# A batched matmul whose TensorE loop is aligned to a code block and given one empty first turn

## The chip, the cores and the metric

One core of one Trainium2 (trn2) chip. The metric is device time in microseconds (us) of one execution; lower is better. PE is TensorE and PEld its weight load, DVE is VectorE, ACT is ScalarE, POOL is GpSimd, SP issues the transfers; a q after a name (PEq, SPq) is the engine's sequencer, whose records are its branches, register operations and waits. The span is the time from the first to the last instruction of the profiled run. PSUM is the memory that PE's results go to here. The clock in a window is the share of PE's full clock that was granted. A block is what one packet of queue 8 brings, 16,384 bytes of code in these traces.

## The reference

```python
def reference(x, weight):      # x: 8 x 16 x 256 x 512, weight: 8 x 16 x 512 x 384, float32
    return np.matmul(x, weight).astype(np.float32)
```

128 independent products. 168 MB are read and 50 MB written.

## The kernel before

The batches are done in 32 groups of four. For each group SP loads x and the weights in float32, ACT casts x to bf16, DVE casts the weights in eight pieces, PE transposes x (16 instructions), DVE copies the transposed x out of PSUM, PE multiplies in four quarters of 32 matmuls each, ACT copies each quarter out, SP stores. Everything is synchronised with counting semaphores, and the engines run loops of their own, PE with two groups a turn. Cut to what the change and the argument touch:

```python
G = 4; T = 4; XS, WS, OS = 2, 4, 4; PT, PO = 4, 2; LAG = 4; BIAS = 8   # T quarters, PO accumulators

def load(e, t, U, s):                       # SP; group n = t*U + s
    n = t * U + s
    if not isinstance(n, int) or n >= XS:
        e.wait_ge(x_cast, n + (1 - XS))     # ACT's cast has freed the x buffer
    e.dma_start(x_sb[s % XS][:], ...)
    ...                                     # two halves of the weights, each after a wait on w_cast

def prepare(e, t, U, s):                    # DVE
    ...                                     # 8 weight casts, then T copies x_t <- pt

def multiply(e, t, U, s):                   # PE
    n = t * U + s
    e.wait_ge(x_cast, n + 1)
    for q in range(T):
        e.wait_ge(t_copied, n * T + (q + 1 - PT + BIAS))
        ...                                 # 4 transposes
    e.wait_ge(w_cast, n * (G * S) + G * S)
    for q in range(T):
        e.wait_ge(t_copied, n * T + (q + 1 + BIAS))
        e.wait_ge(o_copied, n * T + (q + 1 - PO + BIAS))
        ...                                 # 32 matmuls, then p_made += 1

def on_tensor(e):
    U = 2
    e.sem_inc(t_made, BIAS); e.sem_inc(p_made, BIAS)
    e.wait_ge(id_done, 2)
    with e.Fori(0, NG // U) as t:           # 16 turns
        for s in range(U):
            multiply(e, t, U, s)

def on_scalar(e):                           # copies of quarters 0, 1; cast of the next x; copies 2, 3
    ...
```

## Time and profile before

| | kernel before |
|---|---|
| time, median of 3 runs | 519.71 us (519.63 to 519.82) |
| span of the profiled run | 518.0 us |
| transfers | 218.16 MB, mean 421 GB/s, in the middle 428 to 429 |
| PE, DVE, ACT busy | 61%, 63%, 41% |
| code fetched for PE after the start (queue 8) | 2 packets of 16 KiB, at 29.2 and 37.9 us |

Transfers take the whole span, no engine is busy over two thirds of it. The prediction below shows the lines. In order of time: start, duration, engine, line, operation, count, and in brackets the idle time before and what ended it.

```profile
8.89 3.70 ACT L130 CAST x_bf<-x_sb 128x2048 bf16<-128x2048 f32 x2 [6.28 <-DMA x_sb<-in_x_dram]
12.56 7.86 DVE L148 CAST w_bf<-w_sb 64x1536 bf16<-64x1536 f32 x8 [12.56 <-DMA w_sb<-in_weight_dram]
...
12.72 3.68 PE L167 MATMUL pt<-identity,x_bf 128*128 128x128 f32 x16 [12.72 <-ACT x_bf L130]
```

PE's first transposes start 0.13 us after ACT's first cast ends (8.89 + 3.70). PE isn't late.

### The profile page before, as it was taken

Reading aid. Unit: us, or ns where it says so; the run is one execution under the profiler, and the core shown is the slowest. Engines: PE = TensorE matmul, PEld = TensorE weight load, DVE = VectorE, ACT = ScalarE, POOL = GpSimd, SP = SyncE. Lnnn points to the kernel's source line nnn. Section 1 sums busy time; section 2 is a strip of 40 time slices with the busy share of each in tenths; the row PEclk is TensorE's granted clock in tenths of the full one; section 3 lists DMA queues with packets and bytes.
Section 4 is the critical chain, followed back from the end, with each engine's and each line's share of the span. In section 5 each row is a group of like instructions: output and inputs, shape, how many; then the busy total and the mean of one; then the engine's idle time right before and its main releaser. Section 6 shows DMA issues by size and latency. Waiting matters only on the chain.

```text
span 518.0 us, 11228 instructions
## 1 busy us (share of the span) xinstructions
PE 315.0 (61%) x4608; PEld 198.0 (38%) x4608; DVE 323.9 (63%) x384; ACT 212.8 (41%) x193; POOL 0.7 (0%) x6
## 2 busy tenths in 40 slices
PE   0685775476655676555756557665566655675654
PEld 0453443343433443333434334343344333343432
DVE  0878867655577555775556765557755577555670
ACT  3073643455234552335542345423455234553242
POOL 0000000000000000000000000000000000000000
PEclk9798976888668776868786687768777787878687
DMA  8999999999999999999999999999999999999995
GB/s 337 430 424 428 426 429 427 430 428 427 430 429 426 431 425 430 428 430 432 426 427 429 430 433 425 427 430 428 432 429 427 427 430 430 430 429 424 432 428 229
DMA packets 18868, 218.16 MB, mean 421 GB/s; under 512 B 2096, under 2 KB 2096, under 8 KB 2608
## 3 DMA queue, kind: packets, MB, share of 16 engines
q1 hardware_dynamic: 18864, 218.11, 99.2%
q8 instruction: 2, 0.03, 0.0%
q14 instruction: 2, 0.02, 0.0%
HBM read 167.77 MB, written 50.33 MB: 421 GB/s over the span
## 4 chain that ended last, share of the span: by engine, by line
DMA 82%; DVE 13%; issue 2%; PE 2%; SPq 1%; ACT 0%; DVEq 0%
DMA w_sb<-in_weight_dram 82%; DVE w_bf L148 13%; PE po L181 2%; SPq L108 0%; SPq L100 0%; ACT out_sb L195 0%; DVE x_t L154 0%; DVEq L143 0%; DVEq L225 0%; SPq L287 0%; SPq L54 0%
## 5 line engine op out<-in xcount | busy, mean ns | idle before, releaser
L148 DVE CAST w_bf<-w_sb 64x1536 bf16<-64x1536 f32 x256 | 244.4, 955 | 179.4 <-DMA w_sb<-in_weight_dram 172.3
L181 PE MATMUL po<-w_bf,x_t 128*32 128x384 bf16 x4096 | 233.5, 402 | 122.2 <-DVE x_t L154 122.2
L195 ACT COPY out_sb<-po 128x768 f32<-128x768 f32 x128 | 99.4, 803 | 291.0 <-PE po L181 291.0
L181 PEld LDWEIGHTS po<-w_bf,x_t 128*32 128x32 bf16 x4096 | 125.8, 117 | 227.0 <-DVE x_t L154 131.7
L167 PE MATMUL pt<-identity,x_bf 128*128 128x128 f32 x512 | 81.5, 322 | 73.4 <-ACT x_bf L130 73.4
L130 ACT CAST x_bf<-x_sb 128x2048 bf16<-128x2048 f32 x64 | 118.5, 1902 | 6.3 <-DMA x_sb<-in_x_dram 6.3
L167 PEld LDWEIGHTS pt<-identity,x_bf 128*128 128x128 f32 x512 | 72.2, 212 | 85.2 <-issue 85.2
L154 DVE COPY x_t<-pt 128x1024 bf16<-128x1024 bf16 x128 | 79.5, 682 | 1.0
L130 ACT ACT_TABLE_LOAD x1 | 1.3, 1283 | 1.3 <-PEq L231 1.3
masks.py:199 POOL TENSOR_SCALAR_AFFINE_SELECT identity<-identity 128x128 f32<-128x128 f32 x1 | 0.3, 293 | 0.2 <-POOL identity L201 0.2
L201 POOL MEMSET identity<- 128x128 f32 x1 | 0.2, 205 | 0.5 <-SPq L54 0.5
L276 POOL MEMSET const-uint8-127<- 128x1 uint8 x1 | 0.1, 103 | 0.0
L276 POOL MEMSET const-bfloat16-1.0<- 128x1 bf16 x1 | 0.1, 102 | 0.0
L276 POOL MEMSET const-float32-0.0<- 128x1 f32 x1 | 0.1, 99 | 0.2 <-issue 0.2
L276 POOL MEMSET const-float32-1.0<- 128x1 f32 x1 | 0.1, 99 | 0.0
## 6 DMA issues: line engine op xcount, KB each, us to landing
w_sb<-in_weight_dram SPq DMA_DIRECT2D x64, 1536.0 KB, 27.6
x_sb<-in_x_dram SPq DMA_DIRECT2D x32, 2048.0 KB, 25.9
out_dram<-out_sb SPq DMA_DIRECT2D x31, 1536.0 KB, 30.5
out_dram<-out_sb SPq DMA_DIRECT2D x4, 384.0 KB, 4.1
```

The source lines that it names most:

```text
L130: ins = e.copy(out=x_bf[s % BS][:, :, h], in_=x_sb[s % XS][:].rearrange("p r (q s c) -> p r s q c", s=S, c=KO)[:, :, h],)
L148: e.tensor_copy(out=w_bf[(s * G + d * D + a) % WBS][h * HP : (h + 1) * HP], in_=w_sb[slot][a * HP : (a + 1) * HP, h * KO : (h + 1) * KO, : ...
L154: e.tensor_copy(out=x_t[s % TS][:, 2 * q : 2 * q + 2], in_=pt[(s * T + q) % PT][:].bitcast(bf16),).then_inc(t_copied, 1)
L167: ins = e.transpose(pt[(s * T + q) % PT][:, rr, h, :], words[:, 2 * q + rr, h :: KO // 2], identity[:],)
L181: ins = e.matmul(po[(s * T + q) % PO][mine, rr, :N], x_t[s % TS][:, 2 * q + rr, ko // 2, mine, ko % 2], w_bf[(s * G + i) % WBS][:, ko, :], ...
L195: e.copy(out=out_sb[s % OS][:, 2 * q : 2 * q + 2, :], in_=po[(s * T + q) % PO][:, :, :N],).then_inc(o_copied, 1)
L201: e.memset(identity[:], 0.0).then_inc(id_done, 1)
L276: nc = _bacc.Bacc("TRN2", target_bir_lowering=False, num_devices=1)
```

## The change

The intent is that PE's code lies at a known place (the loop head at slot 0 of a block, as the call asks) and that the loop's last block has been fetched before the work starts: one more turn, the first, skips both bodies and only jumps through. Since the counter now starts one later, all counts move by LEAD = 2 groups.

```diff
-    BIAS = 8
+    BIAS = 16
+    LEAD = 2
...
-            e.wait_ge(x_cast, n + (1 - XS))
+            e.wait_ge(x_cast, n + (1 - XS + LEAD))
...                                     (w_cast, t_copied, o_copied shifted too; multiply split
                                         into transpose and multiply, the latter one quarter q a call)
     def on_vector(e):
+        e.sem_inc(w_cast, LEAD * G * S)
     def on_scalar(e):
+        e.sem_inc(x_cast, LEAD)
...
-        e.wait_ge(id_done, 2)
-        with e.Fori(0, NG // U) as t:
-            for s in range(U):
-                multiply(e, t, U, s)
+        pe = mybir.EngineType.PE
+        with nc.Fori(
+            0, NG // U + 1, engines=OrderedEngineSet([pe]), head_slot={pe: 0}
+        ) as t:
+            with e.If(t > 0):
+                e.wait_ge(id_done, 2)
+                for s in range(U):
+                    transpose(e, t, U, s)
+                    for q in range(T if s == 0 else T // 2):
+                        multiply(e, t, U, s, q)
+            with e.If(t > 0):
+                for q in range(T // 2, T):
+                    multiply(e, t, U, U - 1, q)
```

## The prediction

The clock that it calls full in the group at 33.55 us was 1.00 (33.5 to 39 us).

> **What bounds the kernel now.** I read the slices first, then the chain that ended last, then the waits, then the order in time of one group of four batches, and the sequencer's records in the trace last.
>
> ```profile
> DMA  8999999999999999999999999999999999999995
> GB/s 337 430 424 428 426 429 427 430 428 427 430 429 426 431 425 430 428 430 432 426 427 429 430 433 425 427 430 428 432 429 427 427 430 430 430 429 424 432 428 229
> ```
>
> The transfers are busy in every slice, at a rate that hardly moves from slice 2 to slice 39. Only the first and the last slice are lower. The same by stage (columns: window, its length, busy time and count of PE, PEld, DVE, ACT, POOL, granted clock, DMA share, GB/s):
>
> ```profile
> 0.00:30.00 30.00, 11.77 (x144) 7.46 (x144) 15.04 (x18) 9.22 (x7) 0.70 (x6) 0.89 0.94 390
> ...
> 238.00:490.00 252.00, 155.43 (x2232) 97.06 (x2228) 161.94 (x192) 103.11 (x95) 0.00 (x0) 0.76 1.01 429
> 490.00:518.00 28.00, 14.31 (x232) 8.37 (x224) 10.12 (x12) 9.13 (x10) 0.00 (x0) 0.80 0.80 337
> ```
>
> The page counts 218.16 MB in all. At about 428.5 GB/s, the rate of the middle, they take 509 us, and the span is 518.0 us. The other 9 us are at the two ends: 30 us at 390 GB/s lose 30 x (1 - 390/428.5) = 2.7 us, and 28 us at 337 lose 6.0 us. No change of TensorE's code can get at the 509, and the nine left are 1.7% of the time.
>
> The chain that ended last says the same:
>
> ```profile
> DMA 82%; DVE 13%; issue 2%; PE 2%; SPq 1%; ACT 0%; DVEq 0%
> ```
>
> PE's 2% is one piece, 8.12 us from 502.48 us, the matmuls of the last group after the last weights. In all other groups PE isn't on it. What PE itself waits for:
>
> ```profile
> PE po L181 <- DVE x_t L154: 122.2, 32, 4.8
> PE pt L167 <- ACT x_bf L130: 73.4, 32, 12.7
> ```
>
> Each of the 32 groups has two waits, for data both times: the transposes (L167) for ScalarE's cast of x, the matmuls (L181) for VectorE's first copy of x_t, which stands behind the weight casts and so behind the weights' transfer. Two groups in order of time, which are one turn's second half and the next turn's first:
>
> ```profile
> 278.80 7.30 PE L181 MATMUL po<-w_bf,x_t 128*32 128x384 bf16 x128 [4.25 <-DVE x_t L154]
> ...
> 281.60 0.80 ACT L195 COPY out_sb<-po 128x768 f32<-128x768 f32 x1 [8.81 <-PE po L181]
> ...
> 284.25 3.70 ACT L130 CAST x_bf<-x_sb 128x2048 bf16<-128x2048 f32 x2
> 286.04 7.86 DVE L148 CAST w_bf<-w_sb 64x1536 bf16<-64x1536 f32 x8 [5.50 <-DMA w_sb<-in_weight_dram]
> ...
> 288.08 2.64 PE L167 MATMUL pt<-identity,x_bf 128*128 128x128 f32 x16 [1.99 <-ACT x_bf L130]
> ```
>
> The loop's back edge lies between 286.10 (278.80 + 7.30) and 288.08 us. PE idles 1.99 us there, and ScalarE's cast ends at 287.95, 0.13 us before the transposes. In the middle of a turn, where there is no branch, the gap is the same (1.98 us before the transposes at 271.52). So the back edge costs nothing today.
>
> [...]
>
> ```profile
> q8 instruction: 2, 0.03, 0.0%
> q14 instruction: 2, 0.02, 0.0%
> ```
>
> Queue 8 moved two packets of 16,384 bytes, at 29.2 us (1,061 ns) and 37.9 us (1,108 ns), the end of the first and of the second group. I take them to be PE's[...]. [...] a turn has 32 x 2 instructions of transposes, 256 x 2 of matmuls and some 21 others, about 597[...], yet nothing is fetched on queue 8 after 39 us in 15 more turns. The loop is resident already. [...] here the loop's compare-and-branch takes 208 to 224 ns taken and 76 not taken (the last), so I use these. [...]
>
> **The change, part by part.** The order of the transposes and matmuls doesn't change at all: a turn still does group 2t and group 2t+1, and only the last two quarters of the odd group's matmuls stand in a block of their own behind a second test. DVE, ACT and SP have the same instructions and the same waits; the constants (BIAS 16, LEAD 2) only shift counts for a counter t that starts one later, and two semaphore increments at the start set them.
>
> *Alignment.* Loop head at slot 0 instead of somewhere: 7 instructions longer, about 604[...]. It was resident before, so 0 us in the steady state.
>
> *The first, empty turn.* It tests twice, counts, and jumps back: four instructions, and perhaps one or two fetches. [...] PE stood ready at 1.86 us (its first register operation), and its first transposes wait for x until 12.7 us. Two fetches of 1.1 us and four branches of 0.2 us are an estimated 3 us of 10.8 us free. On the path: 0.
>
> *What it saves.* The fetches at 29.2 and 37.9 us. The second falls into the second group's matmuls, 5.38 us from 33.55; two groups on, at 59.02, with no fetch, they take 5.38 too. The first falls before transposes that wait for ScalarE (cast ends at 30.96, transposes at 31.09). So both are hidden today: saved 0.
>
> *The tests inside a turn.* Per turn I count seven more sequencer instructions: compare-and-branch and a branch twice, two register operations more for the second block's waits, and one semaphore wait for the identity. One follows another about 0.1 us apart in the trace, 0.28 us after a taken branch. Five come between the second and third quarter: an estimated 0.4 to 0.75 us. There the sequencer is held in any case: the third quarter waits until ScalarE has emptied the first of the two accumulators. In the group shown it asked at 281.77 and was released at 282.43, and the quarter's first matmul came at 283.33. In the group at 33.55, when the clock was full: 35.15, 35.92, 36.16. In the last group, the only one where PE is on the chain: 505.46, 506.18, 507.58. So 0.66 to 0.77 us of waiting to take it up, plus 1.4 us of lead in the group that counts. Path: 0, at most 0.1. The remaining ones lie at the back edge, where the sequencer is done at 285.24 and waits until 287.95: 2.7 us free, some 0.5 needed.
>
> *Sum.* 0 to 0.1 us in the last group, 0 elsewhere: 519.7 + 0.05, about 519.8.
>
> **Rivals.** *The loop gets fetched again in each turn*[...]. Three blocks of 16 KiB in 16 turns are 0.79 MB, 1.8 us at 428.5 GB/s, and three stalls of 1.1 us per turn on PE. PE has 2 us before the transposes and up to 4.8 before the matmuls, so most of it stays hidden: some 521.5 us; all of it on the path would be 16 x 3.3 = 53 us more. Against it: the kernel before does not refetch with a head at an arbitrary slot, and the body is hardly longer.
>
> *The fetch is worth something*, in timed runs or by a chain that I don't see: at most its two packets, 2.2 us, so 517.5. Against it: neither is beside an idle stretch of PE that ends late.
>
> *PE's small delays reach the transfers.* There is a way: matmuls, ScalarE's copies, its next cast of x, and only then the issue of the next load of x, for which the queue waits long:
>
> ```profile
> SPq L100 <- ACT x_bf L130: 259.1, 30, 10.2
> ```
>
> But a weight load is issued 27.6 us (median) before it lands, while its 1.57 MB need 3.7 us: over 20 us of other transfers are queued ahead. A delay of 0.5 us shortens the queue and doesn't empty it. At the worst it adds to the last group: 520.3.
>
> **Range and chances.** The three times of before lie within 0.2 us. All mechanisms on the path give 0 to 0.1 us, the rivals -2.2 and +0.6 to +1.8; I put 8 of 10 on 518.8 to 520.8. Faster by 2% means 509.3, which is the transfer time alone without either end: 1%. Slower by 2% means 10.4 us more, 0.65 us on the path in each turn, which only steady refetching could do: 2%.
>
> **What would show it.** After the change: GB/s the same in the middle slices; DMA again some 82% of the chain; some 116 instructions more on PE (16 x 7 + 4) in a total of 11,228 before; packets of queue 8 in the first 12 us instead of at 29 and 38 us, and none later; the transposes again 1.9 to 2.0 us after the matmuls before them, released by ScalarE; the last group's matmuls 8.1 us. I am wrong if queue 8 has packets in each turn, if "PE pt" waits for issue rather than for ScalarE, if a gap over 0.2 us opens between the last group's second and third quarter, or if slices in the middle fall under 424 GB/s.

## The result, and the profile after

519.76 us median (519.50 to 520.07, four runs) against 519.67 us of the kernel before in the same rounds (519.47 to 519.82). The ratio is 1.0002, with a 95% interval of 0.9985 to 1.0020. The two are the same.

The page of the kernel after: the transfers by slice, the fetch queue and the chain that ended last.

```profile
DMA  8999999999999999999999999999999999999995
GB/s 332 427 428 426 428 427 429 431 429 424 430 432 428 431 425 430 429 430 429 428 428 431 425 434 428 427 427 430 431 432 425 429 429 430 431 428 426 431 428 233
...
q8 instruction: 3, 0.05, 0.0%
...
DMA 78%; DVE 13%; PE 3%; issue 3%; SPq 1%; ACT 1%; DVEq 0%; ACTq 0%
```

The rate is what it was. DMA's share of the chain is 78% where the prediction had some 82% again. Queue 8 moved three blocks, at 6.2, 11.8 and 17.3 us, and none later; the third missed the first 12 us that were forecast. PE's waits after (us in total, times, longest):

```profile
PE po L187 <- DVE x_t L157: 119.5, 31, 4.4
PE pt L170 <- ACT x_bf L133: 59.9, 31, 2.0
PE pt L170 <- issue: 15.0, 1, 15.0
```

31 of the 32 transposes still wait for ACT. One doesn't, the first, which waits for PE's own sequencer. The start, in order of time:

```profile
9.93 3.70 ACT L133 CAST x_bf<-x_sb 128x2048 bf16<-128x2048 f32 x2 [7.23 <-DMA x_sb<-in_x_dram]
...
13.85 7.86 DVE L151 CAST w_bf<-w_sb 64x1536 bf16<-64x1536 f32 x8 [13.85 <-DMA w_sb<-in_weight_dram]
14.98 3.27 PEld L170 LDWEIGHTS pt<-identity,x_bf 128*128 128x128 f32 x16 [14.98 <-issue]
14.99 3.47 PE L170 MATMUL pt<-identity,x_bf 128*128 128x128 f32 x16 [14.99 <-issue]
...
22.48 8.25 PE L187 MATMUL po<-w_bf,x_t 128*32 128x384 bf16 x128 [4.02 <-DVE x_t L157]
```

Two things differ from before. ACT's cast ended at 13.63 and the transposes began at 14.99, 1.36 us late. And x itself came 1.04 us later (cast at 9.93, was 8.89), the weights 1.29 us later (13.85, was 12.56). The sequencer's own records in the trace, which no view of the page lists, show the cause of the first (start and duration in ns):

```
 1979  6561  COMPARE_BRANCH  first test of the empty turn
 8598  5516  COMPARE_BRANCH  second test
14172    42  ALU_OP          count
14275   229  COMPARE_BRANCH  back to the head
14656    77  COMPARE_BRANCH  first test of the first real turn (falls through)
```

The empty turn took over 12 us, nearly all of it in two jumps. A packet of queue 8 lies within each (6.22 to 7.19 and 11.79 to 12.78 us), so I read them as waits for a target that wasn't in yet. The turn was hidden by what PE would have waited for in any case: the weight casts end at 13.85 + 7.86 = 21.71 us, and the matmuls start only after them, with 4.02 us of idle time on PE.

The second has a cause that the landings show. Each transfer leaves 16 reports of landing in the trace (2,096 for 131 transfers), and the kernel waits for all 16; I take them as one from each of the 16 DMA engines that the page counts. For the first load of x, fifteen reports came by 8.53 us and the last at 8.86 in the kernel before; in the kernel after fifteen came by 8.68 and the last at 9.91. For the first weights after, fourteen came by 12.39, and two at 13.58 and 13.82. One fetch (6.22 us, 965 ns long) had gone by before the first, two before the second. The second load of x, after the third fetch, has three late reports (thirteen by 20.97, then 22.16, 22.23 and 22.24). So each packet of code seems to hold one engine, each time another, for its 1 us (965 to 1,006 ns), and every load in flight waits for that engine. That is a reading, as the trace names no engine.

### The profile page after: what moved, and what is told of

It is laid out like the page before. It is cut to its first block, busy times and chain, and to the rows that moved or that the text cites. A ratio compares the mean times of both kernels' runs of the same rounds, so it can differ in the third digit from the quotient of the medians.

```text
span 517.9 us, 11305 instructions
## 1 busy us (share of the span) xinstructions
PE 315.2 (61%) x4608; PEld 197.7 (38%) x4608; DVE 323.9 (63%) x384; ACT 212.6 (41%) x193; POOL 0.7 (0%) x6
## 2 busy tenths in 40 slices
DMA packets 18869, 218.18 MB, mean 421 GB/s; under 512 B 2096, under 2 KB 2096, under 8 KB 2608
## 4 chain that ended last, share of the span: by engine, by line
DMA 78%; DVE 13%; PE 3%; issue 3%; SPq 1%; ACT 1%; DVEq 0%; ACTq 0%
DMA w_sb<-in_weight_dram 78%; DVE w_bf L151 13%; PE po L187 3%; ACT x_bf L133 0%; DVE x_t L157 0%; SPq L111 0%; SPq L103 0%; ACT out_sb L201 0%; SPq L110 0%; DVEq L232 0%; ACTq L131 0%; DVEq L146 0%; DVEq L156 0%; ACTq L200 0%; SPq L305 0%
## 5 line engine op out<-in xcount | busy, mean ns | idle before, releaser
L187 PE MATMUL po<-w_bf,x_t 128*32 128x384 bf16 x4096 | 232.5, 401 | 119.6 <-DVE x_t L157 119.5
L187 PEld LDWEIGHTS po<-w_bf,x_t 128*32 128x32 bf16 x4096 | 124.3, 117 | 224.8 <-DVE x_t L157 129.1
L170 PE MATMUL pt<-identity,x_bf 128*128 128x128 f32 x512 | 82.7, 325 | 74.9 <-ACT x_bf L133 59.9
L170 PEld LDWEIGHTS pt<-identity,x_bf 128*128 128x128 f32 x512 | 73.4, 213 | 86.8 <-issue 86.8
```

The lines of the kernel that those rows point to most:

```text
L170: ins = e.transpose(pt[(s * T + q) % PT][:, rr, h, :], words[:, 2 * q + rr, h :: KO // 2], identity[:],)
L187: ins = e.matmul(po[(s * T + q) % PO][mine, rr, :N], x_t[s % TS][:, 2 * q + rr, ko // 2, mine, ko % 2], w_bf[(s * G + i) % WBS][:, ko, :], ...
```

## The experiments

The ones that edit the kernel after are compared with the kernel before too; the result found these two the same.

**Alignment alone.** The kernel before, with only the loop call changed.

```diff
-        with e.Fori(0, NG // U) as t:
+        with nc.Fori(0, NG // U, engines=OrderedEngineSet([pe]), head_slot={pe: 0}) as t:
```

> The kernel before with its TensorE loop aligned to slot 0 of a block, no empty turn and no tests in the turn. Theory (the transfers set the time, PE's code placement is hidden): 519.7 us, within 0.8; no compare-and-branch over 0.3 us; the first transposes start within 0.2 us of the end of ScalarE's first cast; two or three 16 KiB packets on queue 8, all after 12 us or so, none later in the loop. Rival (alignment does something by itself which the empty turn then takes back): the time differs from the kernel before by more than 1 us.

519.61 us against 519.64, ratio 0.9998 (0.9982 to 1.0015). The longest branch was 301 ns, the one onto the aligned head; the transposes began at 13.61, 0.13 us after the cast's end. Queue 8 had packets at 6.1, 32.3 and 40.4 us, so the expectation "all after 12 us" missed by one. That one again came with a late x (cast at 9.78) although PE's work was not held up. Alignment does nothing to the time, and a late first x goes with a fetch, not with the empty turn.

**The empty turn without alignment.**

```diff
-            0, NG // U + 1, engines=OrderedEngineSet([pe]), head_slot={pe: 0}
+            0, NG // U + 1, engines=OrderedEngineSet([pe])
```

> The changed kernel without the alignment. In the changed kernel the first turn's two jumps took 6.6 and 5.5 us. Theory (they wait for blocks of code that aren't in yet, wherever the head lies): the first turn's compare-and-branches still sum to 5 to 13 us, and the time is 519.8 us, within 0.8. Rival (the alignment brought them on): they sum to less than 1 us and the first transposes start within 0.2 us of the end of the first cast.

519.69 us against 519.64, ratio 1.0003 (0.9986 to 1.0020). The empty turn's first jump took 6,887 ns, the second only 233 (its target was in), the jump back 437: 7.6 us in all, in the expected range. The transposes began at 13.65, 0.13 us after ACT's cast (9.82 + 3.70), so that half of the rival's expectation held too: one long jump (7.6 us with the rest of the turn) fits into the wait for x, two (12.5 us) don't. Why there is one here and two there was not shown; no run shows the slots. x came late again (9.82), with a fetch at 6.1 us, the first of five on queue 8 (the last at 39.8 us).

**A quiet start.** The loads wait until the empty turn is over.

```diff
     def on_sync(e):
         U = OS
+        e.wait_ge(turned, 1)
...
             with e.If(t > 0):
                 e.wait_ge(id_done, 2)
+                e.sem_inc(turned, 1)
```

> The changed kernel with the first loads held back until TensorE has done its empty turn, so that its code is fetched while no data moves. Theory (a fetch is short but queues behind the data, so 4 to 5 us of each 5.5 to 6.6 us jump is queueing): each of the two jumps takes 1.5 to 2.5 us, the first load is issued at about 5 to 6 us instead of 1 us, and the whole is 4 to 5 us longer, about 524. Rival (a jump to a block that isn't in costs 5.5 to 6.6 us whatever the transfers do): the jumps stay that long, the loads start at about 14.5 us and the whole takes about 533 us.

527.69 us against 519.64, ratio 1.0154 (1.0137 to 1.0171). The two jumps took 3,321 and 3,116 ns, between what theory and rival said: with no data moving, a miss costs 3.1 to 3.3 us, and under load 5.5 to 6.9. Jump by jump against the kernel after (6,561 and 5,516 ns), 2.4 to 3.2 us, about half, come with the data. The packets show where: here they start 0.5 and 0.7 us after the jump asks, in the kernel after 4.2 and 3.2 us; in both the jump ends 1.3 us after its packet. The first load:

```profile
9.22 0.39 SPq L104 DMA_DIRECT2D x_sb<-in_x_dram  x1
```

It was issued at 9.22 instead of 0.97 us, 8.25 us later, and the whole took 8.05 us longer. The delay of the transfers was paid almost one for one here. The same 12 us of PE in the changed kernel, beside the transfers, cost nothing.

**A pause of PE in every turn.** To measure how much PE can lose per turn: 40 increments of an unused semaphore ahead of the third quarter, about 0.15 us each, 6.1 us a turn.

```diff
             with e.If(t > 0):
+                for _ in range(40):
+                    e.sem_inc(idle, 1)
                 for q in range(T // 2, T):
```

> The changed kernel with 40 increments of an unused semaphore ahead of the third quarter of each turn's odd group, about 6 us of TensorE's sequencer per turn, 96 us in all. Theory (delays of PE in the loop only shorten the queue of transfers; only the last turn's counts): 4 to 5 us longer, about 524.5; the GB/s of the middle slices stay at 424 to 434. Rival (they reach the transfers through ScalarE's cast and the issue of the next x): 30 to 90 us longer, over 550, with lower GB/s all along.

524.88 us against 519.64, ratio 1.0105 (1.0088 to 1.0122): 5.2 us for 16 x 6.1 = 98 us of pauses. PE's waits:

```profile
PE po L188 <- DVE x_t L158: 76.9, 19, 6.3
PE po L188 <- issue: 73.5, 16, 5.2
...
PE pt L171 <- ACT x_bf L134: 34.9, 16, 3.0
```

The 73.5 us of new waiting took the place of old: waits for x_t fell from 119.5 to 76.9 us, waits for the cast from 59.9 to 34.9, together 67.6 us less. The middle windows of the trace have 428 and 429 GB/s, as before. The cost isn't quite the last turn's alone: the last weights' load was issued at 472.3 us, in the kernel after at 469.9, and their casts began at 496.25 instead of 493.74. So 2.5 us of delay did reach the last loads, at an unchanged rate, and the last turn's pause adds 6.1; of these 8.6 us the end hides 3.6, as from ACT's last copy to the end it takes 3.8 us and not 7.4. PE's seven instructions more per turn, of which I estimated 0.5 us, are a small part of such a pause.

**Twice the pause.** 80 increments, 12.2 us a turn, otherwise the same.

> As the pause of 6 us, with 80 increments: some 12 us per turn, 193 us in all. The pause of 6 us cost 5.2 us in the whole. Counted from the kernel before, PE's and ScalarE's loop over a group is about 12.6 us (cast 3.7, first transposes and copy about 2.3, half of the matmuls 5.1, a copy and the gaps) against 16.0 us that its transfers need, and over a turn some 25 to 28 of 32 us. Theory (there are only 4 to 7 us per turn to hide in): the pause of 12 us no longer fits, each turn gets 3 to 8 us longer, 570 to 650 us, and the GB/s falls in all slices. Rival (the queue of 20 us of transfers takes up any pause of this size): only the last turn counts, about 531 us.

529.90 us against 519.62, ratio 1.0203 (1.0188 to 1.0219). My theory fell and the rival stood: 196 us of pauses cost 10.3 us, which is less than the last turn's own 12.2. The page:

```profile
PE 285.4 (54%) x4608; PEld 188.4 (36%) x4608; DVE 324.2 (61%) x384; ACT 216.0 (41%) x193; POOL 0.7 (0%) x6
...
GB/s 335 426 428 431 423 429 428 431 430 424 427 432 427 430 428 432 425 428 429 429 435 421 430 431 429 430 429 428 427 430 431 429 427 431 428 429 429 429 271 63
...
PE 35%; issue 32%; DMA 17%; ACT 9%; DVE 5%; SPq 0%; ACTq 0%; DVEq 0%
```

The rate holds at 421 to 435 from slice 2 to slice 38. But the chain that ended last is mostly PE and its pauses now, and PE's waits for x_t are down to 10.4 us in all: 12 us is about all the slack that a turn has. A longer pause was not run.

My count had been wrong in two ways. I had put the first half of a group's matmuls at 5.1 us, their time when they start at half clock (0.50 was granted from 502 to 508 us of the kernel before); in this run many follow the transposes with hardly a gap, and the whole group takes 5.38 us (at 272.74 us in this trace), and PE's busy time falls from 315 to 285 us. And I had counted the pause as if ACT's next cast stood behind it, when the cast hangs on the first two quarters and runs beside the pause.

**A loop that doesn't stay in.** The change is about code that must be fetched, so a kernel in which it should have to be, by my estimate: the kernel before, PE unrolled to eight groups a turn, some 2,390 instructions.

```diff
     def on_tensor(e):
+        U = 8
         with e.Fori(0, NG // U) as t:
```

> The kernel before with TensorE's loop unrolled to eight groups a turn: four turns of some 2,390 instructions[...]. It should have to be fetched in each turn: 35 to 40 packets of 16 KiB on queue 8 in place of 2 (if there are only about 10, it was held after all). Theory (a fetch is 16 KiB among 218 MB, and a jump back that waits 5 to 7 us for its block is taken up by the queue of transfers): 37 x 16 KiB is 0.6 MB, 1.4 us; 519.7 to 521.5 us. Rival (a fetch holds one of the DMA engines for its 1 us, and every transfer waits for its slowest engine, as the first x did, which landed 0.9 us later wherever a fetch came at 6 us): about 1 us each, 30 to 40 us longer, 550 us or more.

524.02 us against 519.62, ratio 1.0082 (1.0066 to 1.0097). Fetch queue, and PE's waits:

```profile
q8 instruction: 42, 0.69, 0.5%
...
PE pt L167 <- ACT x_bf L130: 67.0, 29, 12.8
PE pt L167 <- issue: 15.5, 3, 5.4
```

42 packets in place of 2: the loop is now fetched in each turn. The three jumps back stall, with branches of 5,861 to 6,312 ns and 5.4 us of idle PE at the most. The extra is 4.4 us for 40 packets, 0.11 us each: neither the 1.4 us of the bytes nor the 1 us each of the rival. The size between them is explained in good part by engine time: 0.5% of the 16 engines' span of 522.4 us, as the page has it, is 2.6 us. My estimate from that: one engine is held for 1 us, which is a sixteenth of that for the whole, if the fetches go round. That they go round is read from the landings above (one, two and three late reports after as many fetches); the trace names no engine.

**Sixteen groups a turn.**

> As the one with eight groups a turn, but sixteen: two turns of some 4,780 instructions[...], and one jump back only. About 38 packets on queue 8, in an even stream. Theory: 519.7 to 521.5 us, with matmuls as dense as before [...]. Rival (a fetch costs about 1 us of every transfer in flight): 550 us or more. If eight groups are slower than this one by more than 1 us, it is the jumps back and not the fetches.

523.28 us against 519.62, ratio 1.0069 (1.0053 to 1.0084).

```profile
q8 instruction: 38, 0.62, 0.5%
```

With one jump back instead of three, and four packets fewer, it is 0.74 us faster than with eight groups. So most of the cost (3.7 us) goes with the fetches and not with the jumps. It builds up in the loads: the last weight casts began at 497.62 us, 3.8 us later than in the kernel before. The fetches' engine time, an estimated 38 x 1.06 / 16 = 2.5 us, with the 1,061 ns of a packet in the kernel before, leaves about 1 us that I can't place. No run has an unrolled loop that still fits, so a cost of unrolling itself isn't ruled out.

**Sharing out the last group's casts.** The prediction put PE on the path in the last group alone. If so, starting it earlier should pay. DVE's last eight weight casts, 7.86 us, were shared among three engines: five, ACT one, POOL two.

```diff
+    ON_DVE = [(0,0,0), (0,0,1), (0,1,0), (0,1,1), (1,0,0)]
+    ON_ACT = [(1,0,1)]
+    ON_POOL = [(1,1,0), (1,1,1)]
-        with e.Fori(0, NG // U) as t:       # on DVE
+        with e.Fori(0, NG // U - 1) as t:
...
+        prepare(e, 0, NG, NG - 2)
+        prepare(e, 0, NG, NG - 1, last=True)   # DVE's share, then it waits for the others'
...                                             (ACT and POOL cast their shares)
```

> The kernel before with the last group's eight weight casts shared out: five on VectorE, one on ScalarE, two on GpSimd. Theory (the end after the last load is where TensorE's chain does count): the last matmuls start about 3 us earlier, at 499.5 instead of 502.5 us, and the whole is 2 to 3 us shorter, about 517.3. Rival (the stores still in the queue then set the end, and the loads before): no more than 0.5 us shorter. The rest must be the same: same GB/s in slices 2 to 38.

519.71 us against 519.62, ratio 1.0001 (0.9987 to 1.0015). The matmuls began only 0.2 us earlier, since GpSimd's casts were slow, 3.70 us for two where DVE's take 0.96 us each:

```profile
497.25 3.70 POOL L145 CAST w_bf<-w_sb 64x1536 bf16<-64x1536 f32 x2 [495.56 <-DMA w_sb<-in_weight_dram]
```

So it didn't test its theory, and was run again with six, one and one.

> As the first sharing of the last group's casts, which ended no sooner since GpSimd's two casts took 1.6 and 2.1 us from 497.25 us, when the second half of the weights was in: now VectorE has six, ScalarE one, GpSimd one. Theory (TensorE's chain counts after the last load): VectorE's casts end at about 499.8 instead of 501.7 us, the last matmuls begin about 2 us earlier, at 500.3, and the whole is 1 to 2 us shorter, about 518.3. Rival (up to 508 us the stores keep the transfers full, so that part of the end is transfer time too): 0 to 0.5 us shorter, within the noise.

519.59 us against 519.63, ratio 0.9999 (0.9986 to 1.0013). This time the end of the compute did move. The matmuls began at 501.48 us, 1.0 us earlier and not the 2 expected, and ran 0.5 us shorter. ACT's last copy, before and here:

```profile
510.63 0.80 ACT out_sb L195
```
```profile
509.11 0.80 ACT L219 COPY out_sb<-po 128x768 f32<-128x768 f32 x1 [0.50 <-PE po L205]
```

It is 1.52 us earlier, and the time is the same; the interval leaves room for a gain of 0.7 us at most. Both still move 371 to 406 GB/s from 505 to 510 us (columns: window, length, busy time and count of PE, PEld, DVE, ACT, POOL, clock, DMA share, GB/s); before, then here:

```profile
505.00:510.00 5.00, 5.00 (x92) 2.79 (x88) 0.00 (x0) 2.27 (x3) 0.00 (x0) 0.70 0.89 371
510.00:515.00 5.00, 0.57 (x16) 0.12 (x8) 0.00 (x0) 0.93 (x2) 0.00 (x0) 0.98 0.55 221
```
```profile
505.00:510.00 5.00, 4.05 (x88) 2.26 (x80) 0.00 (x0) 2.54 (x4) 0.00 (x0) 0.90 0.98 406
510.00:515.00 5.00, 0.00 (x0) 0.00 (x0) 0.00 (x0) 0.00 (x0) 0.00 (x0) 0.78 0.46 185
```

More was moved early and less late, but the last bytes came no sooner. The last reports of landing are at 513.88, 514.06, 514.72, 515.65 and 516.56 us before and at 513.59, 514.09, 514.52, 515.44 and 516.35 here. The last three are 0.9 us apart in both, after all the others. That looks like one engine with a backlog, working off its share of the last pieces by itself; in the store before the last group's, fifteen reports had come by 510.36 us and the sixteenth came at 512.87. The trace names no engine, so this stays a reading and not a proof. The runs do show that about 1.5 us of PE's end have slack: compute that ended that much sooner gained nothing that can be measured. So no version came out that beats both kernels.

## Why the prediction was right

*The bound.* Right. The middle slices keep 424 to 434 GB/s. Where the loads start 8.25 us later the time grows by 8.05 us; where PE loses 98 us it grows by 5.2. That places the bound in the transfers, not in PE.

*Alignment, 0 us.* Right: 519.61 us with alignment alone. Residency, the reason given, holds: no packet on queue 8 after 17.3 us in the kernel after or after 40.4 in the aligned one. The control is the loop of some 2,390 instructions, 42 packets and 4.4 us.

*The empty turn, "an estimated 3 us of 10.8 us free".* The conclusion (0 on the path) held, the term was off by four: it took 12.5 us, from 1.98 to 14.5 us. I had taken the packet's 1.1 us on the DMA engine for the time that PE waits. That wait is 3.1 to 3.3 us with nothing else moving and 5.5 to 6.6 here. It overran the 10.8 us, and the first transposes came 1.36 us late. It was saved by the next wait, for the weights: 4.02 us of idle PE were left. The prediction had not asked for that second margin, so this part came out right by luck.

*What it saves, 0 us.* Right. The fetches at 29.2 and 37.9 us are gone, and nothing got faster. Not foreseen: the early fetches delayed the first loads by 0.9 to 1.3 us, each, as it seems, through one engine of sixteen. They are not seen in the time. The kernel before has two fetches as well, and the last group's weight casts began at 493.74 us in the one after and 493.85 in the one before.

*The tests inside a turn.* Right in sign, smaller than estimated: from the record of the second test to the third quarter's own register operation the sequencer takes 0.25 us (36.166 to 36.415 us), not 0.4 to 0.75, since a test that falls through takes 68 ns. The third quarter's matmuls follow the second's 1.30 us after these began, with no gap; nor is there one in the last group. I foresaw 116 instructions more on PE. The records have 54, as the second block has no separate waits for the accumulators and PE's records hold no unconditional branch (only 53 compare-and-branches, before 17). The page has 77 more in all; 21 of the others are register operations on SP, whose instructions were forecast to stay the same.

*The last group, "the only one where PE is on the chain".* Here a step was wrong that did no harm. The chain of waits does go through PE there, but compute that ended 1.5 us earlier brought nothing. The kernel after itself shows it: its last group took 7.25 instead of 8.12 us of PE time, with the clock coming up sooner (0.95 was granted from 506 to 508 us, before 0.50), and the spans are 517.9 and 518.0 us.

*The rivals.* Refetching in each turn didn't occur; where it was forced, it cost 4.4 us, more than the 1.8 us of its bytes. That run had 3 stalls and not the 48 behind the 53 us, so it doesn't test that figure; the pauses bear on it, as 16 of 6.1 us cost 5.2 in all. "PE's small delays reach the transfers" fell in that the rate held, even at 12 us a turn; but pauses of 6 us did bring the last loads 2.5 us later.

## What to carry to other kernels

Before tuning an engine's code layout, ask what that engine waits for: here PE's idle time of some 12.7 us a turn ((518.0 - 315.0) / 16) swallowed pauses of 12 us, though hardly more, while 8 us of later loads cost 8. A jump to a block that wasn't in cost 3.1 to 3.3 us with no data moving and 5.5 to 6.9 us under load, not the microsecond that its packet takes, so an empty turn that is to fetch code ahead must have several times that hidden behind a wait. Where transfers are the bound, keep the loop small enough to stay in (about 604 instructions did, with no packet after 17.3 us in 16 turns; about 2,390 didn't, with 42 packets): each refetched block cost 0.1 us of the whole. The chain that ended last names the last link, not the slack beside it; shorten the link to see whether it binds.
